# An RWKV-7 block with adaptive norm, followed by a second block, on one Trainium2 core: silu(c) and five modulation sums made a stage earlier, and a 16x16 inverse in another form

## The chip, the cores and the metric

The kernel runs on one core of a Trainium2 chip as a single launch. The metric is device time in microseconds (us); the time before is 2746.52 us, the median of three runs (2742.11 to 2747.39). TensorE (PE in the profile, with its weight loads as PEld), VectorE (DVE), ScalarE (ACT) and GpSimd (POOL) compute; SyncE (SP) issues nearly all DMAs. Each engine works off its own list of instructions in the order in which the program was written, and waits where an operand is not there.

## The reference, cut to what matters

One token block of 256 x 2048 in fp32 goes through a conditioned RWKV-7 block with a feed-forward part, and then through a second block (attention, a gated recurrence, an MLP). The change lies wholly within the first half of the first block:

```python
mod = jax.nn.silu(c) @ ada_w + ada_b                       # 2048 x (6 x 2048)
sh_m, sc_m, g_m, sh_f, sc_f, g_f = split(mod + ada_table)  # six vectors of 2048
h = rms(x) * (1 + sc_m) + sh_m
y = rwkv7(h)                                               # r, k, v, w, a, g products, scan, group norm, @ w_o
x = x + g_m * rms(y)
h = rms(x) * (1 + sc_f) + sh_f                             # then the conv feed-forward part, gated by g_f
```

`sh_m` and `sc_m` are needed before anything else. The other four vectors (2048 x 8192 of `ada_w`, 32 MB) are needed only after `y @ w_o`. Here they are called the modulation sums: 128 units, one for each half h of `c` and each block ch of 128 outputs; 96 of them are made before the feed-forward part. In the scan, 256 steps are done in chunks of 16: for each chunk and head a unit lower triangle of 16 x 16 has to be inverted, 64 such triangles for each group of four heads.

## The kernel before, in words

All products are fp32, made from two halves each of weights and of activations (`hi`, `lo`), three matmuls to a product. A weight comes as a `raw` tile of 512 KB by a DMA on SP's queue (`wdma`, L167), ACT casts its high half (`spl`, L183), DVE subtracts to get the low half (`spl`, L184), and PE multiplies. The list of all weight tiles is fixed, and so many of them are loaded ahead as there are `raw` buffers; each load waits for the buffer that an earlier split gives back.

The stages, by the times of the profiled execution:

- **start** (0 to about 165 us, `start`): `x` is loaded (L709), normed and transposed. At the same time 64 tiles of 512 KB of `ada_w` (`ada`, L451) give `sh_m` and `sc_m` in eight groups of eight, by DVE (L471, L474) and PE (L469). Seven `ada` tiles are in flight.
- **mixes** (to about 217 us, `mixes`): the remaining `r` products in two halves of six weights each (L864 to L866), four low-rank hidden vectors (`hidden`, tanh on ACT at L846), and the token-shift mixes for the next products.
- **jit** (217 to about 630 us, `jit`): eight groups g of four heads each. A group makes its k, v, w, a products (L1043 to L1045) slot by slot; at each of 64 slots the function `pump` takes one step of the three streams of earlier work: s0 (decay, keys; ends in L1079 to L1104 and the tiles `LA`, `LB`), s1 (chunk matrices L1141, the inverse L1170 to L1182, its spread over partitions through DRAM images `imgT` and `imgP` into `Tm` and `Pm`, L1214), s2 (the scan chain, and the group norm at L1287 to L1299).
- **wo** (630 to about 830 us): `y @ w_o` in two halves p = 0, 1 of twelve weights, with the last group's streams between.

The modulation sums are a generator, `ada_sums` (L481). It broadcasts a row of `c` over the partitions into `sb` by a DMA on POOL's queue (L497, 512 KB), makes silu(c) by a tanh on ACT (L500) and a multiply on DVE (L501), and then each step makes one sum: DVE multiplies a 512 KB tile `adat` (L492, a DMA on SP) by `sb` and adds up the row (L507). When the unit's half changes, the row and the silu come again. Where the caller calls `next`, there the step stands in all engines' lists, the loads among them. In `mixes` the number of sums is N0 = 0. In `jit` there are N3 = 61, at the slots of the table `SLOT3` (four in group 0, where two go to the row and the silu, seven in group 1, nine in each later group; the second half's row and silu take two slots of the seventh group). One `adat` tile is in flight. In `wo` the other 35 come by `self.pump(1 + p)` for each weight, with five tiles in flight in `scratch` and `ab`.

The inverse (L1172 to L1178) solves the triangle column by column: for t = 1 to 15 DVE multiplies the t x t corner P by column t of G into `tG` (L1176) and adds up along the row into column t (L1178). At t = 4, 7, 9, 11 and 13 it yields to the other streams. L1182 then transposes the result.

The function `wnext` hands out the split weights; `self.deferred` is a list of small pieces of work that the next `flush` in a product loop emits, in order.

Of the kernel before, what the change touches and what calls it, by code (L numbers as in the profile page):

```python
# [97 lines left out]
class Kern:  # L98
# [8 lines left out]
    ASH = [4, 7, 9, 10]  # L107
    N0 = 0
    N3 = 61
    SLOT3 = [[40, 51, 57, 63], [12, 18, 25, 33, 40, 51, 63]] + [[7, 12, 18, 25, 30, 33, 40, 51, 63]] * 6  # L110

# [369 lines left out]
    def ada_sums(self, units, sb, bufs, half=None, lag=0):  # L481

        nc = self.nc
        nb, nxt = len(bufs), 0

        def load(end):
            nonlocal nxt
            while nxt < min(end, len(units)):  # L490
                h, ch = units[nxt]
                nc.sync.dma_start(out=bufs[nxt % nb], in_=self.A["adat"][h, ch])  # L492
                nxt += 1
        load(nb if half is not None else nb - 1)
        for n, (h, ch) in enumerate(units):
            if h != half:
                nc.gpsimd.dma_start(out=sb, in_=self.A["rows"][4, h * 1024:h * 1024 + 1024].partition_broadcast(128))  # L497
                yield
                t = bufs[(n + nb - 1) % nb]
                nc.scalar.activation(out=t, in_=sb, func=AF.Tanh, scale=0.5)  # L500
                nc.vector.scalar_tensor_tensor(out=sb, in0=t, scalar=1.0, in1=sb, op0=ALU.add, op1=ALU.mult)  # L501
                half = h
                load(n + nb)
                yield
            load(n + nb - lag)
            t = bufs[n % nb]
            nc.vector.scalar_tensor_tensor(out=t, in0=t, scalar=0.5, in1=sb, op0=ALU.mult, op1=ALU.mult,  # L507
                                           accum_out=self.asum[:, h, ch:ch + 1])
            if nb == 1 and n + 1 < len(units) and units[n + 1][0] == h:
                load(n + 2)  # L510
            yield
# [138 lines left out]
    def rwkv(self):  # L650
        nc, A, tc = self.nc, self.A, self.tc
        with ExitStack() as top:
            hidp = top.enter_context(tc.tile_pool(name="hid", bufs=1))
            self.hid = hidp.tile([128, 4, 2, S], F32R, name="hid")
            with tc.tile_pool(name="hpool", bufs=1) as hp:
                self.vec0 = hp.tile([128, NVEC - NV1], F32, name="vec0")
# [45 lines left out]
    def start(self):  # L702
# [5 lines left out]
        for tb in range(2):  # L708
            nc.sync.dma_start(out=x0[:, tb, :], in_=A["x"][tb * 128:tb * 128 + 128, :])  # L709
        self.ada_start(range(8), lambda: wk.tile([128, 1024], F32, tag="ada", bufs=7, name="ada")[:], 7)  # L710
        acc = wk.tile([128, 2, 512], F32, name="acc")
# [99 lines left out]
        pp = prep(0)  # L811
        for g in range(1, 8):
            for i, _ in enumerate(ada(g)):
                if g > 1 or i > self.LAG:
                    next(pp, None)
                product()
            if g == 1:
                for _ in pp:
                    pass
            pp = prep(g)  # L820
# [19 lines left out]
    def mixes(self, xr):  # L840
# [3 lines left out]
        def hidden(i, p, func, scale):  # L844
            t = wk.tile([128, S], F32, tag="lt", bufs=2, name="lt")
            nc.scalar.activation(out=t, in_=p, func=AF.Tanh, scale=scale) if func else nc.scalar.copy(out=t, in_=p)  # L846
            if scale == 0.5:
                nc.vector.tensor_scalar(out=t, in0=t, scalar1=0.5, scalar2=0.5, op0=ALU.mult, op1=ALU.add)
            self.hilo(hid[:, i, 0, :], hid[:, i, 1, :], t)
        sums = self.ada_sums(self.aunits[:self.N0], wk.tile([128, 1024], F32, name="sb")[:],  # L850
                             [wk.tile([128, 1024], F32, name=f"ab{i}")[:] for i in range(4)])
        self.aunits = self.aunits[self.N0:]
        next(sums, None)
        for i in range(4):
            self.deferred.append(lambda i=i: hidden(i, self.lb[i // 2][:, i % 2, :], i != 1, 1.0 if i < 2 else 0.5))
        ps = [self.bank(b, (128, S), "r") for b in (7, 0, 1, 2, 3, 4)]
        for half in range(2):
            for n, ft in enumerate(range(10, 16)):
                hi, lo = self.wnext()
                for k in range(8):  # L860
# [8 lines left out]
                    if k == 5 and n:  # L869
                        self.pump()  # L870
                    if k in (1, 4) and n + half:
                        next(sums, None)
# [72 lines left out]
    def jit(self):  # L945
# [12 lines left out]
        n3 = self.N3  # L958
        ab = self.ab = self.sp.tile([128, 2, 1024], F32, name="ab")
        s3 = self.ada_sums(self.aunits[:n3], ab[:, 0, :], [ab[:, 1, :]])  # L960
        self.aunits = self.aunits[n3:]
# [146 lines left out]
    def s1(self, g):  # L1108
# [64 lines left out]
        nc.vector.memset(P[:].rearrange("p a b -> p (a b)")[:, 0:256:17], 1.0)  # L1173
        for t in range(1, 16):
            tv = tmp[:, 0:t * t].rearrange("p (a b) -> p a b", a=t)
            nc.vector.tensor_tensor(out=tv, in0=P[:, 0:t, 0:t], in1=G[:, 0:t, t].unsqueeze(1).broadcast_to([64, t, t]),  # L1176
                                    op=ALU.mult)
            nc.vector.tensor_reduce(out=P[:, 0:t, t], in_=tv, axis=AX.X, op=ALU.add)  # L1178
            if t in (4, 7, 9, 11, 13):
                yield next(at)  # L1180
# [123 lines left out]
    def wo(self):  # L1304
# [9 lines left out]
        ngm = sum(ch < 16 for _, ch in self.aunits)  # L1314
        self.side = [self.ada_sums(self.aunits, self.ab[:, 0, :], v + [self.ab[:, 1, :]], 1, 1)]
        gate = self.ada_gate(0, "b_gm", "t_gm", self.G, self.Af[:], lambda: self.misc((128, 4, 128), "gr"))
# [12 lines left out]
        for p in range(2):  # L1329
# [6 lines left out]
            for kc in range(12):  # L1336
                if p == 0 and kc < 11:
                    split(kc + 1)
                hi, lo = self.wnext()
                self.pump(1 + p)  # L1340
                if p == 1 and kc % 2 and kc < 10:
# [564 lines left out]
```

## Time and profile before

| what | value |
|---|---|
| median of three runs | 2746.52 us |
| profiled execution | 2750.28 us, of which the span from first to last instruction is 2748.2 us |
| PE busy | 2607.2 us (95% of the span) |
| DVE, ACT busy | 1771.8 us (64%), 1340.5 us (49%) |
| chain that ended last | PE 84%, ACT 6%, DVE 5%, DMA 3%, issue 2% |
| mean granted TensorE clock | 0.981 of full speed |

A granted clock of 1.00 is TensorE's upper level of 2.4 GHz, 0.5 its lower level of 1.2 GHz; a stretch with 0.54 ran almost wholly at the lower one. The share of the whole span says little about a change that touches the first 830 us only: each stage has its own limit, and the stretch, its waits and its chain have to be read apart. From about 830 us on the program is the same before and after.

### The profile page before, as it was taken

How to read it: one execution, taken by the hardware profiler on the slowest of the kernel's cores; microseconds unless marked ns; L12 is line 12 of the kernel's file. 1: busy time of each engine (PE TensorE's matmuls, PEld its weight loads, DVE VectorE, ACT ScalarE, POOL GpSimd, SP SyncE). 2: the span in 40 equal slices, each digit the busy share in tenths (PEclk: the TensorE clock that was granted, in tenths of full speed). 3: DMA queues.
4: the chain of work that ended last, by engine and by line, in shares of the span. 5: the costliest groups of instructions: out<-in, count | busy, mean ns of one | idle time of the engine just before them, and what ended most of it. 6: DMA issues, size and time to landing. Idle time of an engine off the chain costs nothing.

```text
span 2748.2 us, 47787 instructions
## 1 busy us (share of the span) xinstructions
PE 2607.2 (95%) x19345; PEld 2379.6 (87%) x19345; DVE 1771.8 (64%) x2842; ACT 1340.5 (49%) x2202; POOL 60.0 (2%) x98
## 2 busy tenths in 40 slices
PE   6997899998879999999999899998989999999998
PEld 6997788886659999999888799998789999988886
DVE  6976888887777786666555656665554444455555
ACT  3245565664455444444444555555454444444444
POOL 0000111111000000000000000000000000000000
PEclk9998999999989999999999999999999999999999
DMA  9945555556757785555555544443535555555554
GB/s 337 388 143 173 192 193 186 173 186 206 251 184 265 268 273 174 183 183 184 179 195 193 176 156 138 140 145 118 190 132 184 184 184 182 181 194 194 192 194 159
DMA packets 151084, 532.56 MB, mean 194 GB/s; under 512 B 21328, under 2 KB 21712, under 8 KB 149840
## 3 DMA queue, kind: packets, MB, share of 16 engines
q1 hardware_dynamic: 146640, 515.36, 55.5%
q0 software_dynamic: 3936, 12.06, 1.7%
q8 instruction: 151, 2.47, 0.4%
q10 hardware_dynamic: 288, 2.10, 0.2%
q14 instruction: 69, 0.57, 0.1%
HBM read 523.16 MB, written 6.29 MB: 193 GB/s over the span
## 4 chain that ended last, share of the span: by engine, by line
PE 84%; ACT 6%; DVE 5%; DMA 3%; issue 2%; SPq 0%; DVEq 0%; ACTq 0%; POOLq 0%
PE ta L353 7%; PE ta L354 7%; PE ta L352 7%; PE f L274 6%; PE f L276 6%; PE f L275 6%; PE u L274 4%; PE u L275 4%; PE u L276 4%; PE m L1043 3%; PE m L1044 3%; PE m L1045 3%; PE r L776 2%; DVE spl L184 1%; PE mi L1141 1%
## 5 line engine op out<-in xcount | busy, mean ns | idle before, releaser
L184 DVE TENSOR_TENSOR spl<-raw,spl 128x1024 fp32r<-128x1024 f32 x748 | 913.2, 1222 | 776.7 <-ACT spl L183 773.7
L183 ACT CAST spl<-raw 128x1024 fp32r<-128x1024 f32 x748 | 781.3, 1045 | 860.8 <-PE ta L354 307.4
L274 PE MATMUL f<-yhl,spl 128*128 128x256 f32 x1376 | 390.1, 284 | 0.0
L275 PE MATMUL f<-yhl,spl 128*128 128x256 f32 x1376 | 389.7, 283 | 0.0
L276 PE MATMUL f<-yhl,spl 128*128 128x256 f32 x1376 | 389.7, 283 | 0.0
L352 PE MATMUL ta<-spl,shl 128*128 128x512 f32 x832 | 324.8, 390 | 3.4 <-ACT shl L287 3.4
L353 PE MATMUL ta<-spl,shl 128*128 128x512 f32 x832 | 324.6, 390 | 1.5 <-DVE spl L184 1.5
L354 PE MATMUL ta<-spl,shl 128*128 128x512 f32 x832 | 324.4, 390 | 0.0
L274 PE MATMUL u<-hl,spl 128*128 128x256 f32 x1024 | 290.1, 283 | 0.0
L275 PE MATMUL u<-hl,spl 128*128 128x256 f32 x1024 | 290.0, 283 | 0.0
L276 PE MATMUL u<-hl,spl 128*128 128x256 f32 x1024 | 290.0, 283 | 0.0
L275 PEld LDWEIGHTS f<-yhl,spl 128*128 128x128 f32 x1376 | 264.3, 192 | 0.0
L274 PEld LDWEIGHTS f<-yhl,spl 128*128 128x128 f32 x1376 | 264.3, 192 | 0.0
L276 PEld LDWEIGHTS f<-yhl,spl 128*128 128x128 f32 x1376 | 264.3, 192 | 0.0
L1043 PE MATMUL m<-hl,spl 128*128 128x256 f32 x672 | 200.3, 298 | 0.0
L275 PEld LDWEIGHTS u<-hl,spl 128*128 128x128 f32 x1024 | 196.7, 192 | 0.0
L276 PEld LDWEIGHTS u<-hl,spl 128*128 128x128 f32 x1024 | 196.7, 192 | 0.0
L274 PEld LDWEIGHTS u<-hl,spl 128*128 128x128 f32 x1024 | 196.7, 192 | 0.0
L1044 PE MATMUL m<-hl,spl 128*128 128x256 f32 x672 | 190.5, 283 | 0.0
L1045 PE MATMUL m<-hl,spl 128*128 128x256 f32 x672 | 190.5, 283 | 0.0
L352 PEld LDWEIGHTS ta<-spl,shl 128*128 128x128 f32 x832 | 156.6, 188 | 36.5 <-ACT shl L287 3.8
L353 PEld LDWEIGHTS ta<-spl,shl 128*128 128x128 f32 x832 | 156.6, 188 | 34.6 <-DVE spl L184 2.1
(424 smaller groups left out, 4799.3 us busy)
## 6 DMA issues: line engine op xcount, KB each, us to landing
raw<-in_ffn_in SPq DMA_DIRECT2D x172, 512.0 KB, 4.7
raw<-in_w_up SPq DMA_DIRECT2D x128, 512.0 KB, 3.8
raw<-in_w_down SPq DMA_DIRECT2D x128, 512.0 KB, 4.4
raw<-in_ffn_out SPq DMA_DIRECT2D x86, 512.0 KB, 3.8
raw<-in_w_in SPq DMA_DIRECT2D x84, 512.0 KB, 3.7
raw<-in_w_rkv SPq DMA_DIRECT2D x76, 512.0 KB, 4.4
ab<-in_adat SPq DMA_DIRECT2D x68, 512.0 KB, 3.5
ada<-in_ada SPq DMA_DIRECT2D x64, 512.0 KB, 6.6
```

What stands on the lines that cost most here:

```text
L183: self.nc.scalar.copy(out=hi[:, :n], in_=t[:, :n])
L184: self.nc.vector.tensor_tensor(out=lo[:, :n], in0=t[:, :n], in1=hi[:, :n].bitcast(F32), op=ALU.subtract)
L274: nc.tensor.matmul(out, lhsT=hi[:, w], rhs=xhl[:, 0, kc, :], start=(kc == 0), stop=False)
L275: nc.tensor.matmul(out, lhsT=hi[:, w], rhs=xhl[:, 1, kc, :], start=False, stop=False)
L276: nc.tensor.matmul(out, lhsT=lo[:, w], rhs=xhl[:, 0, kc, :], start=False, stop=(kc == KD - 1))
L352: nc.tensor.matmul(o, lhsT=shl[0][:, t0], rhs=hi[:, w], start=first, stop=False)
L353: nc.tensor.matmul(o, lhsT=shl[0][:, t0], rhs=lo[:, w], start=False, stop=False)
L354: nc.tensor.matmul(o, lhsT=shl[1][:, t0], rhs=hi[:, w], start=False, stop=last)
L776: nc.tensor.matmul(out, lhsT=wd[:, w], rhs=xt[:, g % 2, max(0, min(3, ft - 9)), kc % 2, :], start=False, stop=e)
L1043: nc.tensor.matmul(out, lhsT=hi[:, w], rhs=xhl[:, 0, kc, :], start=(kc == 0), stop=False)
L1044: nc.tensor.matmul(out, lhsT=hi[:, w], rhs=xhl[:, 1, kc, :], start=False, stop=False)
L1045: nc.tensor.matmul(out, lhsT=lo[:, w], rhs=xhl[:, 0, kc, :], start=False, stop=(kc == KD - 1))
```

## The change

Seven edits. `sb` becomes a tile of its own that lives through the whole RWKV part, and its row for the first half of `c` is written in `start`, in the code of the sixth modulation group. The silu of this half is put behind the four hidden vectors in `mixes`, and five sums stand in the first half of its weight loop (N0 = 5), with three tiles for `adat`. `ada_sums` yields right after its first loads when it is handed a finished silu; its callers take that first step at once. Group 0 of `jit` has two slots for sums instead of four, and no silu; since 61 units still follow, the change of halves comes earlier, and the second silu falls on the last slot of the sixth group. In `wo` 30 sums are left, and the second half's steps go 1, 2, 1, 2. `start` has six `ada` tiles instead of seven. The inverse gives the same result in another order: the first row is copied from G, and as soon as column t is finished its part is added to all later columns, n x m elements with n = t + 1 and m = 15 - t.

```diff
-    N0 = 0
+    N0 = 5
     N3 = 61
-    SLOT3 = [[40, 51, 57, 63], [12, 18, 25, 33, 40, 51, 63]] + [[7, 12, 18, 25, 30, 33, 40, 51, 63]] * 6
+    SLOT3 = [[46, 62], [12, 18, 25, 33, 40, 51, 63]] + [[7, 12, 18, 25, 30, 33, 40, 51, 63]] * 6
...
         load(nb if half is not None else nb - 1)
+        if half is not None:
+            yield
         for n, (h, ch) in enumerate(units):
...
             self.hid = hidp.tile([128, 4, 2, S], F32R, name="hid")
+            self.sb = hidp.tile([128, 1024], F32, name="sb")
...
-        self.ada_start(range(8), lambda: wk.tile([128, 1024], F32, tag="ada", bufs=7, name="ada")[:], 7)
+        self.ada_start(range(8), lambda: wk.tile([128, 1024], F32, tag="ada", bufs=6, name="ada")[:], 6)
...
         for g in range(1, 8):
+            if g == 5:
+                nc.gpsimd.dma_start(out=self.sb[:], in_=A["rows"][4, 0:1024].partition_broadcast(128))
...
-        sums = self.ada_sums(self.aunits[:self.N0], wk.tile([128, 1024], F32, name="sb")[:],
-                             [wk.tile([128, 1024], F32, name=f"ab{i}")[:] for i in range(4)])
+        sums = self.ada_sums(self.aunits[:self.N0], self.sb[:],
+                             [wk.tile([128, 1024], F32, name=f"ab{i}")[:] for i in range(3)], 0)
...
+        def silu():
+            t = wk.tile([128, 1024], F32, name="st")
+            nc.scalar.activation(out=t[:], in_=self.sb[:], func=AF.Tanh, scale=0.5)
+            nc.vector.scalar_tensor_tensor(out=self.sb[:], in0=t[:], scalar=1.0, in1=self.sb[:], op0=ALU.add,
+                                           op1=ALU.mult)
+        self.deferred.append(silu)
...
-                    if k in (1, 4) and n + half:
+                    if k == 5 and n:
                         next(sums, None)
...
-        ab = self.ab = self.sp.tile([128, 2, 1024], F32, name="ab")
-        s3 = self.ada_sums(self.aunits[:n3], ab[:, 0, :], [ab[:, 1, :]])
+        ab = self.ab = self.sp.tile([128, 1024], F32, name="ab")
+        s3 = self.ada_sums(self.aunits[:n3], self.sb[:], [ab[:]], 0)
+        next(s3)
...
-        for t in range(1, 16):
-            tv = tmp[:, 0:t * t].rearrange("p (a b) -> p a b", a=t)
-            nc.vector.tensor_tensor(out=tv, in0=P[:, 0:t, 0:t], in1=G[:, 0:t, t].unsqueeze(1).broadcast_to([64, t, t]),
-                                    op=ALU.mult)
-            nc.vector.tensor_reduce(out=P[:, 0:t, t], in_=tv, axis=AX.X, op=ALU.add)
-            if t in (4, 7, 9, 11, 13):
+        nc.vector.tensor_copy(out=P[:, 0, 1:16], in_=G[:, 0, 1:16])
+        for t in range(1, 15):
+
+            n, m = t + 1, 15 - t
+            if m > 1:
+                tv = tmp[:, 0:n * m].rearrange("p (a b) -> p a b", a=n)
+                nc.vector.tensor_tensor(out=tv, in0=P[:, 0:n, t:t + 1].broadcast_to([64, n, m]),
+                                        in1=G[:, t, n:16].unsqueeze(1).broadcast_to([64, n, m]), op=ALU.mult)
+                nc.vector.tensor_tensor(out=P[:, 0:n, n:16], in0=tv, in1=P[:, 0:n, n:16], op=ALU.add)
+            else:
+                nc.vector.scalar_tensor_tensor(out=P[:, 0:n, 15], in0=P[:, 0:n, t], scalar=G[:, t, 15:16],
+                                               in1=P[:, 0:n, 15], op0=ALU.mult, op1=ALU.add)
+            if t in (3, 5, 7, 9, 12):
                 yield next(at)
...
-        self.side = [self.ada_sums(self.aunits, self.ab[:, 0, :], v + [self.ab[:, 1, :]], 1, 1)]
+        self.side = [self.ada_sums(self.aunits, self.sb[:], v + [self.ab[:]], 1, 1)]
+        next(self.side[0])
...
-                self.pump(1 + p)
+                self.pump(1 + kc % 2 * p)
```

The instructions themselves move as follows; the line numbers of the changed kernel are some 2 to 20 higher.

VectorE in group 0 before, from the keys of stream s0 to the first chunk matrices' operand `LA`:

```order
L1090 SCALAR_TENSOR_TENSOR kb<-kb,k 128x8x64
L501 SCALAR_TENSOR_TENSOR ab<-ab 128x1024
L1093 TENSOR_TENSOR kkr<-C,kkr 128x512
L1094 SCALAR_TENSOR_TENSOR kb<-za,kkr 128x8x64
L1099 SCALAR_TENSOR_TENSOR C<-r,vec,kb 128x256 x2
L1104 TENSOR_TENSOR kb<-kb,zw 128x1024
L184 TENSOR_TENSOR spl_2139<-raw_2057,spl_2138 128x1024
L507 SCALAR_TENSOR_TENSOR ab,asum<-ab 128x1024 x2
L184 TENSOR_TENSOR spl_2176<-raw_2088,spl_2175 128x1024
L1118 TENSOR_TENSOR LA<-r,Ep 128x8x64
L1119 SCALAR_TENSOR_TENSOR LA<-kkr,Ep 128x8x64
```

The same place on VectorE in the changed kernel:

```order
L509 SCALAR_TENSOR_TENSOR ab,asum<-ab,sb 128x1024
L184 TENSOR_TENSOR spl_2106<-raw_2032,spl_2105 128x1024
L1093 TENSOR_SCALAR C<-mi_2112 128x512
L1100 TENSOR_SCALAR kb<-za,half 128x4x64 x2
L1103 SCALAR_TENSOR_TENSOR kb<-kb,k 128x8x64
L1106 TENSOR_TENSOR kkr<-C,kkr 128x512
L1107 SCALAR_TENSOR_TENSOR kb<-za,kkr 128x8x64
L1112 SCALAR_TENSOR_TENSOR C<-r,vec,kb 128x256 x2
L1117 TENSOR_TENSOR kb<-kb,zw 128x1024
L184 TENSOR_TENSOR spl_2151<-raw_2071,spl_2150 128x1024
L509 SCALAR_TENSOR_TENSOR ab,asum<-ab,sb 128x1024
L184 TENSOR_TENSOR spl_2186<-raw_2103,spl_2185 128x1024
```

The silu (L501) and one of the two sums ahead of `LA` are gone; the other of the two new sums stands a split earlier, and the two `LA` rows follow the last row shown.

ScalarE where the sixth group ends and the seventh begins, before (`VA`, `VB`: chunk values; `v`: the group's values; `LB`: the copied half of `LA`):

```order
L1206 COPY VB<-mi_5286 64x4x64
L981 COPY v<-pv_5029 128x512
L183 CAST spl_5314<-raw_5174 128x1024
L1121 COPY LB<-LA 64x1024
L1123 COPY ecl<-Ep 128x8
```

and in the changed kernel:

```order
L1226 COPY VB<-mi_5284 64x4x64
L502 ACT_TABLE_LOAD
L502 ACTIVATE ab<-sb 128x1024
L994 COPY v<-pv_5028 128x512
L183 CAST spl_5313<-raw_5173 128x1024
```

A table load and the tanh of the second half's silu now stand ahead of the copy of `v` and of the cast. On VectorE the silu's multiply stands at the same place, where a sum was:

```order
L1117 TENSOR_TENSOR kb<-kb,zw 128x1024
L184 TENSOR_TENSOR spl_5244<-raw_5111,spl_5243 128x1024
L503 SCALAR_TENSOR_TENSOR sb<-ab,sb 128x1024
L1314 TENSOR_TENSOR r<-r,Y 128x512
L1317 SCALAR_TENSOR_TENSOR r<-r,vec,bv 128x256
L1319 SCALAR_TENSOR_TENSOR r<-r,vec,zg 128x256
L1317 SCALAR_TENSOR_TENSOR r<-r,vec,bv 128x256
L1319 SCALAR_TENSOR_TENSOR r<-r,vec,zg 128x256
L184 TENSOR_TENSOR spl_5314<-raw_5173,spl_5313 128x1024
```

The five rows of the group norm, a split and the two `LA` rows come behind it.

SyncE's loads where `wo` begins, before (`scratch<-in_rows`: the row of the norm's gain, 1 MB):

```order
L542 DMA scratch<-in_rows 128x2048
L167 DMA raw_6668<-in_w_o 128x1024
L167 DMA raw_6670<-in_w_o 128x1024
L167 DMA raw_6699<-in_w_o 128x1024
L492 DMA scratch<-in_adat 128x1024 x4
L492 DMA ab<-in_adat 128x1024
```

and in the changed kernel:

```order
L544 DMA scratch<-in_rows 128x2048
L492 DMA scratch<-in_adat 128x1024 x4
L492 DMA ab<-in_adat 128x1024
L167 DMA raw_6669<-in_w_o 128x1024
L167 DMA raw_6671<-in_w_o 128x1024
L167 DMA raw_6700<-in_w_o 128x1024
```

Five loads for the sums have moved ahead of three weights. On POOL the row of `c` for the first half, before the first DMA after `start`, is now the first DMA of the program; it waits for nothing. The second half's row stands between the stores of the sixth group's images (`imgT`, `imgP`) and the loads of its `Tm`. On PE the order is the same in both.

## Rows read from the trace of the kernel before

**Rows 1.** Windows: busy us of each engine (instructions), clock, DMA share, GB/s.
```profile
241.00:258.00 17.00, 8.51 (x30) 6.77 (x31) 11.34 (x17) 3.07 (x5) 0.00 (x0) 0.51 0.49 171
305.00:630.00 325.00, 313.40 (x3403) 266.08 (x3402) 282.72 (x548) 201.09 (x406) 42.93 (x67) 0.99 0.56 187
548.20:551.60 3.40, 3.36 (x16) 3.37 (x17) 1.87 (x4) 1.85 (x5) 0.00 (x0) 0.54 0.76 266
647.10:657.40 10.30, 9.00 (x80) 7.51 (x81) 8.41 (x13) 3.27 (x7) 0.00 (x0) 0.51 0.36 103
```

**Rows 2.** Chain of waits, 0 to 20 us: start us, us, what.
```profile
2.13 6.39 DMA x<-in_x
```

**Rows 3.** DMA view, 60 to 120 us.
```profile
DMA packets 6371, 22.32 MB, mean 372 GB/s; under 512 B 704, under 2 KB 704, under 8 KB 6364
```

**Rows 4.** Tile `ada`, 0 to 170 us: count, ns min/median/max, first and last start.
```profile
L451 SPq DMA_DIRECT2D ada<-in_ada x64: 327/328/1147, 3.1 to 130.8; - x64
...
DMA to landing us min/median/max: 3.2/6.6/12.7
```

**Rows 5.** PE's waits, 165 to 211 us: us in total, times, longest.
```profile
PE r L864 <- ACT spl L183: 1.9, 1, 1.9
```

**Rows 6.** VectorE's timeline in mixes: start, us, instruction [idle before <-releaser].
```profile
184.09 1.23 DVE L184 TENSOR_TENSOR spl<-raw,spl 128x1024 fp32r<-128x1024 f32 x1 [3.18 <-ACT spl L183]
```

**Rows 7.** Chain of waits, 215 to 305 us.
```profile
236.88 1.28 ACT L500
238.18 1.06 ACT ab L500
239.26 1.23 DVE ab L501
...
245.01 1.15 DVE ab L507 x2
246.18 3.23 DMA ab<-in_adat
```

**Rows 8.** VectorE by form, 270 to 288 us: busy us, mean ns of one.
```profile
L1176 DVE TENSOR_TENSOR tG<-PG,G 64x225 f32<-64x225 f32 x1 | 0.5, 548 | 0.0
...
L1176 DVE TENSOR_TENSOR tG<-PG,G 64x64 f32<-64x64 f32 x1 | 0.3, 258 | 0.0
```

**Rows 9.** PE's waits, 211 to 305 us.
```profile
PE mi L1214 <- DMA Tm<-imgT: 3.5, 2, 2.3
```

**Rows 10.** Chain of waits, 515 to 524.5 us.
```profile
518.80 0.59 ACT v L981
```

**Rows 11.** VectorE's timeline, 515 to 526 us.
```profile
517.29 0.69 DVE L1294 TENSOR_TENSOR r<-r,Y 128x512 f32<-128x512 f32 x1 [0.43 <-ACT Y L299]
...
520.37 1.23 DVE L184 TENSOR_TENSOR spl<-raw,spl 128x1024 fp32r<-128x1024 f32 x1 [0.43 <-ACT spl L183]
```

**Rows 12.** PE's timeline: three groups' L1079, and L1141 after the sixth group.
```profile
451.15 0.70 PE L1079 MATMUL mi<-C,cst 128*128 128x512 f32 x1
...
506.39 0.70 PE L1079 MATMUL mi<-C,cst 128*128 128x512 f32 x1
...
522.94 1.13 PE L1141 MATMUL mi<-LA,kb 64*128 64x128 f32 x8 [0.45 <-DVE LA L1119]
...
564.39 0.70 PE L1079 MATMUL mi<-C,cst 128*128 128x512 f32 x1
```

**Rows 13.** Chain of waits, 626 to 660 us.
```profile
637.33 6.43 DMA scratch<-in_adat
...
647.82 0.96 ACT spl L183
...
651.83 3.68 PE mi L1214 x64
```

**Rows 14.** VectorE's waits, 625 to 780 us.
```profile
DVE scratch L507 <- DMA scratch<-in_adat: 12.5, 5, 6.9
```

**Rows 15.** PE's waits, 625 to 780 us.
```profile
PE ch L1253 <- DVE Pm L1234: 3.4, 1, 3.4
```

## The prediction, made before the result was known

> **What bounds the kernel now.** I read the windows first, stage by stage, because 95% busy over the whole span hides where PE stands still. In groups 1 to 7 of jit PE works 313.40 of 325 us at a clock of 0.99 [rows 1]: work taken from VectorE or ScalarE there buys nothing unless PE waits for it. The change can only pay or cost where PE does wait, so I then listed PE's waits by stretch and read the chain of waits through each long one. There are five such places below 830 us: the program's start [rows 2], the turn to the second `r` loop in mixes [rows 5], group 0 [rows 7, 9], the second silu [rows 12], and wo [rows 13 to 15]. After a long gap PE also runs for a while at the lower clock: 17 us at 0.51 in group 0, 3.4 us at 0.54 after the second silu, 10.3 us at 0.51 where wo begins [rows 1]. Such a stretch costs about half of its busy time: 4.2, 1.5 and 4.4 us. After 830 us nothing differs.
>
> All sums below are against the profiled execution (2750.28 us, span 2748.2, so 2.1 us lie around it); the median of the runs is 2746.52, 0.14% less, and I carry the difference over to it unchanged.
>
> **1. The row of silu's input at the start: +1.0.** The row's DMA waits for nothing on POOL, so its 512 KB travel with `x`, on whose landing the first work hangs: 6.39 us for the first megabyte [rows 2]. At 372 GB/s [rows 3] 512 KB take 1.4 us. If the queue has room while `x` starts, it costs 0. I take 1.0, nearer to the full price, as everything in the stage hangs behind `x`. That the row is gone from 218 us helps nothing on its own; there the first sum's tile takes its place.
>
> **2. Six tiles instead of seven: 0.** 57 tiles follow the first seven between 3 and 130.8 us, one per 2.24 us [rows 4]; six in flight leave 13.4 us from a tile's issue to its reuse. Landing takes 6.6 us in the median, 12.7 at worst [rows 4]. The worst is in the first rush, where fewer loads in the queue also land sooner. The price if this cover goes is the third rival.
>
> **3. Mixes: +1.2 (0 to +3).** The tanh (1.06) and the multiply (1.23), priced by the old silu [rows 7], stand behind the hidden vectors and ahead of the next split, exactly where PE already waits 1.9 us for a cast [rows 5]. ScalarE pays first, and VectorE's multiply overlaps the next cast, so the delay is the larger of the two, 1.2, not their sum. Below, 0 if something else is later; above, +3 if the longer gap lengthens the lower clock behind it by a stretch like the short one [rows 1]. The table is the one just used by the hidden vectors, so no load. The five sums fall into VectorE's idle time: a split is 1.23 with 3.18 idle before it [rows 6], and a sum takes 1.15 [rows 7]. If that cover were gone, each would cost 1.15.
>
> **4. Group 0: -10.0 (-5 to -14).** The chain runs from the decay's last activation to `LA`, which L1141 on PE reads. Removed from it [rows 7]: table load, tanh and multiply, 236.88 to 240.49 = 3.6; one of two sums, 1.15; the load of the next `adat` tile, 3.23, since with both sums' tiles fetched far earlier nothing is left to land there. That is 8.0. Against it, the first `adat` tile now stands ahead of a weight, worth up to 1.4 at [rows 3]'s rate, partly repaid by the row that no longer travels there: +0.5. PE's gap ahead of L1141 was what kept the clock low for 17 us; of the 4.2 us lost there I count 1.5, the rest lay inside the waits. The new inverse is shorter by 1.5 us (next item), and PE waits 3.5 us for `Tm` behind it [rows 9]: -1.0 of that. Low end: only the load and the sum count (-4.4) and little else; high end: whole clock loss and whole `Tm` wait.
>
> The table load moves to the next group's tanh, where every later group has one already and PE does not wait.
>
> **5. The inverse elsewhere: 0.** Old: 30 small operations; a 64x64 multiply is 0.258, 64x225 0.548, so 1.8 ns per element of a row [rows 8]. New: a copy, 26 operations of 28 to 64 elements and a last one of 15. The fixed part of an operation is 0.258 - 64 x 0.0018 = 0.14. The multiplies fall from 1240 elements to 650: 1.8 ns on 590 is 1.1, and two operations less are 0.3. The reductions give way to additions in place over the same 650; such an addition is not in the trace, and at half the multiply's slope per element more or less than a reduction it moves the sum by 0.6 either way: -0.8 to -2.0. I take -1.5. From group 2 on PE is the bound [rows 1] and this is worth nothing.
> The Trainium skill (VectorE: DVE Perf Modes, Walkthrough: the 8-slice pipeline in each mode) has fp32 tensor_tensor at one element per cycle of 0.96 GHz, 1.04 ns; the row's 1.8 ns does not agree, probably by the pattern of its operands, which I cannot tell. By the skill's rate the new inverse would be an estimated 1 us shorter still and the total 1 us lower.
>
> **6. The second silu at the end of the sixth group: +3.5 (+1.5 to +6.5).** Before, it cost one group 58.00 us from L1079 to L1079 instead of 55.24 [rows 12]: 2.8, which now goes. Its new place is ahead of the copy of `v` at 518.80 [rows 10]. Load 1.28 and tanh 1.06 from there end at 521.2, the multiply at 522.4. The group norm behind it on VectorE, which began at 517.29, therefore starts 5.1 later; its five operations take until 520.0 before [rows 11], now until 525.1; the split at 520.37 starts at 525.1, and so `LA` comes 4.7 later. PE waited 0.45 there already [rows 12], and its list holds nothing else to do: a gap of 5.1. Behind it I count 3.4 us of lower clock, 1.5 [rows 1]. 4.7 + 1.5 - 2.8 = +3.5. Low: part is caught up before the chain products; high: a stretch as at 647 [rows 1], 4.4. The adat load that now waits for the multiply, and the loads of `Tm` behind the row on POOL, come later by 1 to 4 us, but inside the same gap.
> On tables the row shows the tanh 0.02 us after a load of 1.28 [rows 7]. The Trainium skill (ScalarE: Activation LUTs, What ACT_TABLE_LOAD costs) adds a drain of 1.38 us to each switch; the trace does not show it. With it the term would be +4.9 and the total 1.4 higher.
>
> **7. Where wo begins: -3.0 (-6 to 0).** VectorE's first sum waits 6.9 us for its tile [rows 14], issued at 637.33 behind three weights and landed at 643.76 [rows 13], and everything for `LA` queues behind that sum. Now the five tiles go ahead of the three weights. That alone is 3 x 1.4 = 4.2 us [rows 3], the first tile at 639.5; and the issue no longer waits until the third weight has a buffer, so it is rather 2 us less, 637.5 (an estimate). But the first of the weights lands behind the other four tiles, 5 x 1.4 = 7.0 later: 644.5, where before it had long been there. From its cast to PE's L1214 lie 4.0 us (647.82 to 651.83 [rows 13]), so L1214 starts at about 648.5: 3.3 earlier, not 6.9. The stall moves to the weight. I take 3.0. Low: the clock's 4.4 [rows 1] partly comes back too. High: the first tile lands at 640 or later, and the weight with it.
>
> **8. The rest of wo: -4.0 (-8 to 0).** Five sums less here: 5 x 1.15 of VectorE, and 5 x 1.4 = 7.0 us of DMA; the sums' waits besides the first are 12.5 - 6.9 = 5.6 [rows 14], and the longest wait of PE, 3.4 [rows 15], hangs on VectorE behind them. I count it and half a microsecond at the end.
>
> Sum: 1.0 + 0 + 1.2 - 10.0 + 0 + 3.5 - 3.0 - 4.0 = -11.3: 2739.0 profiled, 2735 for the median. Its own range, by errors of the terms that are independent: 2728 to 2742.
>
> **Rivals.**
> A, *the new gap costs far more*: lower clock after the sixth group lasts as in group 0, 17 us and 8 us lost [rows 1] instead of 1.5. For it: the gap, 5.1, is as long as the longest there. Against: there several gaps followed each other. Total -5: 2742.
> B, *the weights take the place of the sums' tiles*: in group 0 and in wo the loads for the sums go ahead of weights; if those are as tight as it seems, items 7 and 8 give 0 and item 4 loses 1.4: -3: 2743.5. For it: item 7's working; against: VectorE waited 12.5 us for sums' tiles [rows 14], which only then counts for nothing.
> C, *slower: six tiles are too few at the start*. One mechanism: a tile that takes longer than 13.4 us from issue to reuse holds up the next; each microsecond above costs 64/6 = 10.7. At 15.0 us it is +17: 2752. It outweighs the gains from 14.5 us. For it: landing can take 12.7 [rows 4]; against: the median of 6.6 leaves 6.8 for use.
> D, *more comes back*: the clock's loss in group 0 and in wo goes whole, 4.2 + 4.4 less the 1.5 counted: 2728 or below.
>
> **How the numbers follow.** Forecast 0.55, A 0.17, B 0.14, C 0.08, D 0.06. A measurement of this kernel tells differences above about 0.2%, 5.5 us: faster means below 2741.0, slower above 2752.0. Faster: nearly all of the forecast (0.53), D, and somewhat under half of A and B (0.14): 0.73. Slower: C at its price and a little of A and B together: 0.07. Same: 0.20. The range 2722 to 2747 leaves out C and the far ends.
>
> **What would show it.** `LA` in group 0 done about 8 us earlier and hardly any time below full clock between 241 and 258 us of before (4); PE waiting some 5 us at L1141 after the sixth group, and a normal seventh group of 55.2 (6); the first sum in wo no longer waiting, but a gap of 3 to 4 us ahead of the first L1214 (7); one load of `ada` at most that VectorE or PE waits for (2). I am wrong if the start stage grows by over 2 us, if the gap in (6) vanishes, or if the first gap in wo stays as it is.

## The result, and the profile after

The changed kernel takes 2732.64 us (median of five runs, 2730.64 to 2738.36) against 2746.52 (2742.11 to 2747.81). The ratio is 0.9941, 95% interval 0.9927 to 0.9956: faster by 16 us, between 12 and 20; the two medians by themselves are 13.9 us apart. The span of the profiled execution fell from 2748.2 to 2728.9.

PE runs the same instructions in the same order in all kernels here, so one instruction, by its number, can be looked up in two traces, and the difference of its two start times is how far the program is ahead (minus) or behind (plus) there. This table has that shift in us (median over the PE instructions within 3 us of the time named, which is a time of before), and the ends of a stage subtracted give what the stage gained or lost. One execution of each kernel stands behind it.

How far executions of the same instructions differ can be read from two runs further down: the one that changes only the loads of wo is off by -1.5 us in mixes, +3.2 in group 0 and -1.4 from 540 to 575, where its program is still that of before; the one that changes only the start by -0.6 in group 0 and -1.7 at wo's beginning. The last 1900 us, the same in all kernels, lie between -3.4 and +1.6. So a stage's figure is good to 2 or 3 us. Group 0 as in the changed kernel is in six runs, and gains between 6.8 and 8.6 in them.

| us of before | 160 | 210 | 305 | 500 | 540 | 575 | 628 | 660 | 760 | 830 | 2740 |
|---|---|---|---|---|---|---|---|---|---|---|---|
| changed kernel, shift | +0.3 | +1.4 | -6.2 | -6.4 | +1.3 | -2.3 | -2.3 | -8.3 | -16.7 | -18.5 | -19.3 |

Stage by stage against the forecast (from the shifts before rounding):

| stage | forecast | measured |
|---|---|---|
| start | +1.0 | +0.3 |
| mixes | +1.2 | +1.0 |
| group 0 (210 to 305) | -10.0 | -7.5 |
| silu at the end of the sixth group, and the old one gone (500 to 575) | +3.5 | +7.6 - 3.5 = +4.1 |
| wo's beginning (628 to 660) | -3.0 | -6.0 |
| rest of wo (660 to 830) | -4.0 | -10.2 |

The windows that answer to [rows 1] (columns as there):

```profile
241.00:258.00 17.00, 15.21 (x78) 12.87 (x79) 13.40 (x20) 4.20 (x8) 1.18 (x2) 0.70 0.42 147
305.00:630.00 325.00, 310.21 (x3343) 263.05 (x3342) 266.49 (x531) 201.80 (x408) 42.48 (x67) 0.98 0.56 185
521.00:528.00 7.00, 6.93 (x77) 6.39 (x78) 5.42 (x9) 2.50 (x4) 0.00 (x0) 0.50 0.43 152
632.00:640.00 8.00, 7.76 (x23) 5.04 (x23) 5.95 (x10) 2.93 (x6) 0.00 (x0) 0.79 1.02 381
640.00:660.00 20.00, 18.40 (x199) 14.23 (x198) 15.27 (x25) 6.47 (x11) 1.39 (x2) 1.00 0.59 202
700.00:760.00 60.00, 58.73 (x514) 43.87 (x513) 43.97 (x68) 27.37 (x51) 0.00 (x0) 1.00 0.72 247
```

In group 0 PE is busy 15.2 of the 17 us in which it had been busy 8.5, partly still at the lower clock. Where wo begins, the lower clock is gone from 640 to 660 us, but a shorter stretch has come ahead of it: 0.79 from 632 to 640, and 0.50 from 634 to 637. The kernel before had 1.00 there. A new stretch of 7 us at 0.50, the lower level of 1.2 GHz, stands at 521 to 528.

The chain through group 0, which answers to [rows 7] (start, us, what):

```profile
239.56 0.80 DVE C L1112 x2
...
241.52 1.23 DVE spl L184
...
246.36 2.00 PE mi L1154 x8
```

From the decay's activations (236.7 to 238.1) on, no table, no tanh, no sum and no load stand on it any more; PE's first product with `LA` (L1154, the old L1141) starts at 246.3 where it started at 253.1. What PE waits for from 211 to 300 us:

```profile
PE mi L1092 <- ACT C L1089: 5.5, 2, 3.0
PE mi L1234 <- DMA Tm<-imgT: 4.0, 1, 4.0
PE pk L1058 <- DVE spl L184: 3.2, 1, 3.2
PE pv L1058 <- DVE spl L184: 1.7, 1, 1.7
```

The wait for `Tm`, 3.5 before [rows 9], has become 4.0, although the program is 7 us ahead and the inverse is shorter.

The end of the sixth group, answering to [rows 10 to 12] (timeline of the changed kernel: start, us, engine, what; in brackets the idle time before it and what ended it). ScalarE first:

```profile
512.42 1.28 ACT L502 ACT_TABLE_LOAD   x1
513.71 1.06 ACT L502 ACTIVATE ab<-sb 128x1024 f32<-128x1024 f32 x1
514.79 0.58 ACT L994 COPY v<-pv 128x512 f32<-128x512 f32 x1
```

The load of the table and the tanh stand right behind each other, and the copy of PE's result `pv` into `v` follows. VectorE beside them:

```profile
514.80 1.22 DVE L503 SCALAR_TENSOR_TENSOR sb<-ab,sb 128x1024 f32<-128x1024 f32 x1 [6.56 <-ACT ab L502]
515.94 0.68 DVE L1314 TENSOR_TENSOR r<-r,Y 128x512 f32<-128x512 f32 x1
...
518.50 1.22 DVE L184 TENSOR_TENSOR spl<-raw,spl 128x1024 fp32r<-128x1024 f32 x1
```

The multiply by the tanh's result stands ahead of the group norm's and the split's operations. PE in the same stretch:

```profile
500.01 1.13 PE L1092 MATMUL mi<-C,cst 128*128 128x512 f32 x2
...
521.07 1.61 PE L1154 MATMUL mi<-LA,kb 64*128 64x128 f32 x6 [4.94 <-DVE LA L1132]
...
562.14 1.13 PE L1092 MATMUL mi<-C,cst 128*128 128x512 f32 x2
```

VectorE stands idle for 6.56 us until the tanh is done, and five operations of the group norm, a split and `LA` follow. PE's wait of 0.45 us there is now 4.94, and the group takes 62.1 us from L1092 to L1092, where the one before it takes 55.2.

The chain of waits where wo begins, answering to [rows 13]:

```profile
627.73 13.78 DMA raw<-in_w_o
...
641.59 1.05 ACT spl L183
...
645.04 0.61 DVE Y L1245
...
645.69 2.29 PE mi L1234 x64
```

A weight, its cast, VectorE's `Y`, which stands behind the weight's split in VectorE's list, and PE's chunk product with `Y` follow one another. In the kernel before, the longest of PE's waits from 625 to 780 us hung on VectorE behind the first sum:

```profile
PE mi L1141 <- DVE bv L1129: 4.2, 1, 4.2
```

It is gone. PE's waits from 620 to 790 us (total us, count, longest), answering to [rows 15]:

```profile
PE wo L352 <- ACT yhl L287: 3.0, 1, 3.0
PE ch L1280 <- ACT VA L1281: 1.6, 4, 0.4
PE mi L1234 <- DVE Y L1245: 1.6, 1, 1.6
```

VectorE's in the same stretch, answering to [rows 14]:

```profile
DVE scratch L509 <- DMA scratch<-in_adat: 0.9, 2, 0.5
```

The sums' waits for their tiles are down from 12.5 us to 0.9. The chain now runs through a weight that takes 13.8 us to land behind the five tiles; PE waits 1.6 us for what hangs on it. The wait of 3.4 at the chain product after `Pm` [rows 15] is gone too.

### The profile page after: what moved, and what is told of

The parts are those of the page before. It is cut to its first block, busy times and chain, and to the rows that moved or that the text cites. A ratio compares the mean times of both kernels' runs of the same rounds, so it can differ in the third digit from the quotient of the medians.

```text
span 2728.9 us, 47766 instructions
## 1 busy us (share of the span) xinstructions
PE 2602.8 (95%) x19345; PEld 2375.2 (87%) x19345; DVE 1754.7 (64%) x2826; ACT 1341.4 (49%) x2202; POOL 59.5 (2%) x98
## 4 chain that ended last, share of the span: by engine, by line
PE 85%; ACT 6%; DVE 4%; DMA 3%; issue 2%; SPq 0%; POOL 0%; DVEq 0%; ACTq 0%; POOLq 0%
PE ta L353 7%; PE ta L352 7%; PE ta L354 7%; PE f L276 6%; PE f L274 6%; PE f L275 6%; PE u L276 5%; PE u L274 5%; PE u L275 5%; PE m L1056 3%; PE m L1057 3%; PE m L1058 3%; PE mi L1234 1%; PE r L779 1%; PE mi L1154 1%
```

## The experiments

Ratios are to the kernel before. The theories: W, the gain comes from the waits in group 0 and in wo; against it I, the inverse pays in every group.

**The inverse alone.** Edit on the kernel before, cut to its loops (the new inverse whole, and nothing else):

```diff
-        for t in range(1, 16):
...
+        nc.vector.tensor_copy(out=P[:, 0, 1:16], in_=G[:, 0, 1:16])
+        for t in range(1, 15):
...
```

> The kernel before with the new 16x16 inverse and nothing else. Theory W (the gain comes from what stood ahead of PE's products in group 0 and in wo; the inverse is shorter, but PE is the bound or its images come late anyway): VectorE's inverse 1 to 2 us shorter per group, total -1 us, between 0 and -2.5 (ratio 0.9991 to 1.0000). Rival I (the inverse pays in every group, 8 x 1 to 2 us, and is most of the gain): -8 us or more (ratio 0.997 or below).

Measured: 1.0002 (0.9992 to 1.0012). VectorE's groups of the inverse, all eight together, in the kernel before (busy us, mean ns):

```profile
L1176 DVE TENSOR_TENSOR tG<-PG,G 64x1 f32<-64x1 f32 (+14 forms) x120 | 35.4, 295 | 13.7 <-DMA G<-au 10.6
...
L1178 DVE TENSOR_REDUCE PG<-tG 64x1 f32<-64x1 f32 (+14 forms) x120 | 27.9, 232 | 4.3 <-DVE tG L1176 0.3
```

The same groups with the new inverse:

```profile
L1182 DVE TENSOR_TENSOR PG<-tG,PG 64x28 f32<-64x28 f32 (+6 forms) x104 | 21.1, 203 | 3.6
L1180 DVE TENSOR_TENSOR tG<-PG,G 64x28 f32<-64x28 f32 (+6 forms) x104 | 20.9, 201 | 2.8
```

63.3 us became 42.0 and a copy and a last step of 0.17 and 0.24 per group: 2.3 us less per group, and no gain in time that shows. The images show where it went. Median time from issue to landing, in the 15 us around them, in the kernel before (last column, us):

```profile
Tm<-imgT POOLq DMA_DIRECT2D x2, 128.0 KB, 4.1
...
imgT<-tG POOLq DMA_DIRECT2D x1, 64.0 KB, 2.8
```

And with the new inverse alone:

```profile
Tm<-imgT POOLq DMA_DIRECT2D x2, 128.0 KB, 6.2
...
imgT<-tG POOLq DMA_DIRECT2D x1, 64.0 KB, 4.1
```

The store of the image was issued 1.1 us earlier (286.62 for 287.75), closer behind the loads of a sum and a weight (285.4 and 285.8 in both), and took longer; the loads of `Tm` were issued at the same time as before (290.98 for 290.86), now beside the next such pair (290.60 and 291.03) instead of ahead of it (291.74 and 292.17), and landed later. Executions of the old inverse differ too, but less: `Tm` took 5.4 us in the run with only wo's loads changed and 4.0 in the one with six tiles.

**The changed kernel with the old inverse** (the same edit the other way).

> The changed kernel with the inverse of before. Theory W: it keeps nearly the whole gain, -12 to -15 us against before (ratio 0.9945 to 0.9956). Rival I: at least half the gain is lost, -7 us or less (0.9975 or above).

Measured: 0.9952 (0.9940 to 0.9965), 2735.18 us. Nearly the whole gain stays. I is refuted by the pair; two or three microseconds for the inverse within the changed kernel lie inside the intervals.

**Only the loads of wo first.** Edit on the kernel before:

```diff
         load(nb if half is not None else nb - 1)
+        if half is not None:
+            yield
...
         self.side = [self.ada_sums(self.aunits, self.ab[:, 0, :], v + [self.ab[:, 1, :]], 1, 1)]
+        next(self.side[0])
```

> The kernel before, with the five loads for the sums issued ahead of the three weights where wo begins; 35 sums and the old pace of steps stay. Theory W: the first sum no longer waits 6.9 us for its tile, L1141 of the last group comes 4 us earlier and the stretch at the lower clock behind it goes: -6 us, between -4 and -8, all of it between 642 and 660 us of before (ratio 0.9971 to 0.9985). Rival B (the weights take the place of the sums' tiles): the gap moves whole to the weights' casts, 0 to -2 us.

Measured: 0.9984 (0.9974 to 0.9993). The shift goes from +0.6 at 628 us to -5.6 at 660: 6.2 gained at the place named. 1.2 of it are given back by 830 us, where the wait of 3.4 at the chain product [rows 15] is still 2.1:

```profile
PE ch L1255 <- DVE Pm L1236: 2.1, 1, 2.1
```

The whole, 4.4 us by the ratio, is at the low end of W's 4 to 8. Its interval, 1.9 to 7.1, touches the 2 that B allows, the 6.2 at the place named do not: rival B, here and in the prediction, is out.

**The loads of wo last, in the changed kernel.**

```diff
-        next(self.side[0])
...
-                self.pump(1 + kc % 2 * p)
+                self.pump(1 + kc % 2 * p + (p == 0 and kc == 0))
```

> The changed kernel with the five loads of wo behind the three weights again, as before; 30 sums and the new pace stay. Theory W (place of the loads and number of the sums count apart): the first sum waits 6 us and more for its tile again, 6 us come back at wo's beginning, the second half of wo stays as good; +5 to +7 against the changed kernel (ratio to before 0.996 to 0.997). Rival: the two are one effect, and with fewer sums the place does not count: 0 to +2 (0.994 to 0.9955).

Measured: 0.9955 (0.9942 to 0.9969), 2737.42 us, with 0.1 us gained between 628 and 660 instead of 6.0, and 9.7 after it. VectorE's waits in this run, 620 to 790 us:

```profile
DVE scratch L509 <- DMA scratch<-in_adat: 7.3, 1, 7.3
```

PE's waits in the same stretch:

```profile
PE mi L1154 <- DVE bv L1142: 3.0, 1, 3.0
...
PE mi L1234 <- DVE Y L1245: 2.9, 1, 2.9
```

PE's two waits of before (4.2 and 1.3 us) are back, and the later stretch is nearly as good as in the changed kernel (9.7 against 10.2): two separate effects. By time alone this would not be told: +3.8 us by the ratios and +4.8 by the medians fall short of W's +5 to +7, and 0.9955 is the edge of the rival's range. The trace decides against the rival, since the loss stands at wo's beginning alone.

**35 sums in wo, at the old pace.** Edit on the changed kernel:

```diff
-    N3 = 61
+    N3 = 56
...
-                self.pump(1 + kc % 2 * p)
+                self.pump(1 + p)
```

> The changed kernel with N3 = 56 instead of 61 and the old pace of steps in wo, so that wo has 35 sums again, as before, with their loads still ahead of the weights. Theory S (the sums' number and pace in wo cost the second half of wo 9 us, by loads that come too late for VectorE): the 9 us between 660 and 780 us come back, +7 to +10 against the changed kernel (ratio to before 0.9966 to 0.998), with waits of VectorE on tiles of 4 us and more and a PE gap of about 3 us at the chain product after Pm. Rival P (the waits went because wo starts earlier and its streams meet the loads in another phase): 0 to +2 against the changed kernel (0.994 to 0.995).

Measured: 0.9964 (0.9951 to 0.9977), 2739.78 us. Between 660 and 830 us nothing is gained (shift -8.4 to -8.4). VectorE waits 4.9 us for tiles of the sums, its wait from 630 to 800 us:

```profile
DVE scratch L509 <- DMA scratch<-in_adat: 4.9, 3, 2.6
```

PE's waits there, 2.3 us of them at the chain product:

```profile
PE ch L1273 <- DVE Pm L1254: 2.3, 1, 2.3
PE mi L1234 <- DVE Tm L1251: 2.1, 1, 2.1
```

The loss against the changed kernel, 6.3 us by the ratios and 7.1 by the medians, is at the low edge of what S expected, and P's 0 to +2 is out.

**The old pace alone.** Only the second of these two edits; 30 sums.

> The changed kernel with the old pace of steps in wo's second half, two for each weight instead of one and two in turn; 30 sums, which then end six weights earlier. Theory N (the number of the sums counts): at most +2 us against the changed kernel (ratio to before 0.994 to 0.9955). Rival V (the pace counts: two loads and two sums for each weight are more than the queue and VectorE carry there): most of what 35 sums at this pace cost, +5 to +9 (0.996 to 0.9975).

Measured: 0.9960 (0.9947 to 0.9973), 2738.36 us. The stretch 660 to 830 gains 5.1 (-4.9 to -10.0), half of the changed kernel's 10.2, and until 760 us it gains 0.9. VectorE waits 5.7 us for tiles, and the old gap is back:

```profile
PE ch L1273 <- DVE Pm L1254: 3.2, 1, 3.2
```

So the pace is worth about 5 us, 3.2 of them the wait at the chain product, and the five sums less about 5, at the end, where 30 sums are over and 35 are not. The median lost 5.7 us against the changed kernel, 5.2 by the ratios: the low end of what V expected, and more than N's 2.

**The silu elsewhere.** Edit on the changed kernel:

```diff
-    N0 = 5
+    N0 = 7
```

> The changed kernel with seven sums instead of five in mixes (N0 = 7), so that 28 are left in wo and the second half's silu falls two slots of sums earlier, in the midst of the sixth group, where the table of the tanh is loaded already. Theory J (the silu at the end of the sixth group costs a gap of 4 to 5 us at L1141 and a stretch at the lower clock behind it, 6.9 us in all): -5 to -7 us against the changed kernel, so -19 to -21 against before (ratio 0.992 to 0.9935), and the gap at L1141 after the sixth group gone. Rival K (PE is the bound there over the whole group, and the gap is only moved, or two more sums in mixes delay the second loop by as much): 0 to -2 us against the changed kernel (ratio 0.9935 to 0.995).

Measured: 0.9913 (0.9900 to 0.9925), 2723.72 us, 9 us faster than the changed kernel by the medians and 7.7 by the ratios, a little more than J's 5 to 7. The shift stays at -3.9 from 500 to 540 us. PE's timeline at the old gap:

```profile
519.04 1.13 PE L1154 MATMUL mi<-LA,kb 64*128 64x128 f32 x8 [0.45 <-DVE LA L1132]
```

The window behind it (columns as in [rows 1]):

```profile
518.00:526.00 8.00, 7.55 (x105) 6.80 (x105) 7.02 (x12) 2.92 (x6) 0.00 (x0) 1.00 0.38 132
```

The gap of 4.9 us is 0.45 as before, the clock stays up, and the silu costs nothing where it now stands: its tanh runs at 497.4 us without a load, since the decay's tanh has loaded the table at 486.9, and VectorE does the multiply in the place of a sum. J holds, K is refuted. Which counts more, the place or the load that it saves, no run separates. The two further sums in mixes cost nothing that shows (from 160 to 210 us the program falls 1.1 us behind, +2.6 to +3.7, as in the changed kernel, +0.3 to +1.4).

**One further.** `N0 = 8`, which puts the silu right behind the tanh of decay and gate.

> The changed kernel with eight sums in mixes, so that the second half's silu stands at the slot right behind the two tanh of the decay and the key gate in the sixth group, and wo has 27 sums. Theory J (the silu has to stand where its table is loaded and VectorE has slack; sums in mixes are free): like the run with seven, 0.9913, or 1 us better through one sum less in wo (0.990 to 0.992). Rival: eight sums in mixes delay the second loop, or the slot lies on the keys' chain: 2 us and more worse than with seven (0.992 or above).

Measured: 0.9906 (0.9890 to 0.9921), 2724.91 us: the same as with seven, as J said; the sum less in wo shows nothing.

**The first silu alone.** The changed kernel with `N0 = 0`, group 0's sums at slots 57 and 63 as before, and the inverse and wo of before.

> The kernel before with the first half's silu made in mixes (and its row at the program's start, six tiles there), nothing else: no sums in mixes, two sums in group 0 at their old slots, so the second half's silu, the inverse and wo stay as they were. Theory G (in group 0 the silu and the wait for the second sum's tile count apart: 3.6 and 3.2 us): PE's L1141 of the first chunk 3 to 4 us earlier, +2 us at the start and in mixes, in all -1 to -3 us (ratio 0.999 to 0.9996). Rival H (the silu alone is what held group 0; the tile would have been there had the first sum come earlier): -6 us or more (0.998 or below).

Measured: 1.0001 (0.9991 to 1.0012). The chain in group 0:

```profile
243.75 1.15 DVE ab L509 x2
244.92 3.26 DMA ab<-in_adat
...
251.83 2.07 PE mi L1154 x8
```

L1154 comes at 251.8 in place of 253.1, with the program 2.1 us late at 210 us: 3.3 us gained, and the load of 3.26 still there. From 254 to 265 us 2.6 of it go again. That cannot be put down to the silu: the kernels with the inverse alone and with wo's loads alone, which change nothing there, lose 2.4 and 2.7 at the same place, with the clock at 0.91 from 258 to 282 us (0.90 here), where the one execution of the kernel before had 0.99. G was right about the place. The sum, between -2.5 and +3.3 us, is not told apart from G's -1; H is out. What the earlier sum and its landed tile give in group 0 beyond this no run shows by itself; it rests on the chain of waits.

**Six tiles alone.** On the kernel before, `bufs=6` and 6 ahead.

> The kernel before with six tiles in flight in the start stage instead of seven. Theory: nothing, 0 to +1 us (ratio 0.9995 to 1.0005); tiles land before they are needed. Rival C (a tile's turn takes over 13.4 us): each microsecond above costs 10.7, so +5 us or more (1.002 or above).

Measured: 0.9995 (0.9985 to 1.0004). Nothing; rival C is out.

**No sum's load behind the first inverse.** Edit on the run with seven sums:

```diff
-    SLOT3 = [[46, 62], [12, 18, 25, 33, 40, 51, 63]] + ...
+    SLOT3 = [[46, 62], [7, 12, 18, 25, 30, 33, 63]] + ...
```

> The changed kernel with seven sums in mixes, and the seven sums of the second group at slots 7, 12, 18, 25, 30, 33, 63 instead of 12, 18, 25, 33, 40, 51, 63, so that no load for a sum is issued while the first inverse's images are stored and read back. Theory Q (the inverse gains nothing since its images queue behind loads): image to Tm 3 us shorter, PE's wait for Tm in group 0 down from 4 us to 1 to 2, total -2 to -3 us against the run with seven sums (ratio to before 0.990 to 0.9908). Rival: the weights' loads fill the queue all the same, or the earlier sums delay VectorE: 0 to +2 us (0.991 to 0.992).

Measured: 0.9901 (0.9886 to 0.9916), 2722.44 us, the fastest here. PE's wait for `Tm` from 211 to 300 us:

```profile
PE mi L1234 <- DMA Tm<-imgT: 0.4, 1, 0.4
```

The loads of `Tm` (issue to landing, us, last):

```profile
Tm<-imgT POOLq DMA_DIRECT2D x2, 128.0 KB, 3.0
```

3.0 us to landing in place of 6.2, and the wait is gone. No load of 512 KB was issued between 280.0 and 287.6 us, while `Tm`'s loads were issued at 283.7. The interval overlaps that of the run with seven sums, so the gain of 1 to 3 us in total is not told apart by time alone. In the trace group 0 gains 13.0 us instead of 7.5 (the program is 8 us further ahead at 305 us, but 2.3 of these lie in a faster start); 3.2 of them are given back by 308 us, so that about 2 us more than with seven sums are left at 500 us.

**The same with the old inverse.**

> The run with free images, but with the inverse of before. Theory Q (the inverse is on PE's path in group 0 only once nothing else fills the queue behind it): the images are stored 2.3 us later, and PE's wait for Tm grows from 0.4 by 1.5 to 2.5 us; total +2 us (ratio to before 0.9905 to 0.9912). Rival: the wait stays below 1 us, the inverse is off the path there too; 0 (0.990).

Measured: 0.9919 (0.9905 to 0.9933), 2728.38 us. PE's wait for `Tm`:

```profile
PE mi L1227 <- DMA Tm<-imgT: 2.7, 2, 2.3
```

2.3 us more, the time by which the new inverse is shorter: with the sums' loads moved away it is on PE's path, as Q said. By time the two differ by 4.9 us (ratios), more than Q's 2, with intervals that overlap; the wait is the clearer reading.

## Why the prediction was right, step by step

The time fell into the forecast's own range (2728 to 2742 for 2732.6), and the signs of all steps held. The sizes were off in both directions, and the errors cancelled only in part: in the traces the stages add up to -18.5 us at 830 us, not to -11.3, and the profiled execution took 2730.64 us, where 2739.0 was forecast. That the median is nonetheless 2.4 us from the forecast is partly luck: the profiled execution of before (2750.28) was slower than all five timed ones, and that of the changed kernel the fastest of its five. Rival D came true in part, in wo; B and C were refuted by runs, and A's 17 us of lower clock were 7.

- **Start and six tiles (1, 2).** +0.3 instead of +1.0; `x` landed 1.5 us later, but most of it was caught up by 22 us. In the ten kernels here with the row at the start the stage cost between -0.1 and +2.7, about +1 in the middle, so the price was right and this execution a cheap one. Six tiles cost nothing, shown alone; but the first six landed after 9.6 to 12.6 us in that run, the first seven of the kernel before after 9.2 to 12.7: that fewer land sooner did not hold.
- **Mixes (3).** +1.0 against +1.2, at the cast named.
- **Group 0 (4).** `LA` 8 us earlier was right: L1154 moved by 6.8 us, from 1.4 late. Forecast -10.0, measured -7.5. Up to L1154 the step was sound, 8.1 gained for 7.5 forecast; the rest failed: of the 1.5 counted for the clock 0.2 came by 290 us (the clock of the stretch came back only to 0.70), and the wait for `Tm`, which I expected to shrink by 1.0, grew to 4.0 and cost 0.8. How much of the 2.5 is truly missing stays open: the changed group 0 is much alike in six runs, but the old one was 3.2 us slower in the run with only wo's loads changed.
- **Inverse (5).** I had 1.5 us per group and measured 2.3, and priced it at nothing outside group 0, which held. That it would bring 1.0 in group 0 failed: the images stand among loads of 512 KB, and the gain came only with these moved. The Trainium skill (VectorE: DVE Perf Modes, Walkthrough: the 8-slice pipeline in each mode) has 1.04 ns per element for such a multiply. Here 64x28 took 177 ns and 64x64 219, 1.17 ns per element, so for the new form this rate was nearer than the 1.8 ns of the old form's rows.
- **Second silu (6).** A gap of 5.1 was forecast, 4.94 measured, 4.5 more than before for the 4.7 counted. The clock behind it stayed low for 7 us (521 to 528) instead of 3.4; the group lost 6.9 us in all (62.1 less 55.2) where 6.2 were forecast, and so +3.5 became +4.1. The 2.8 us of the old silu were those of one execution: behind its gap of 2.2 us the clock was at 0.54, but 1.00 in three other runs, where it cost 1.4 less. The drain that the Trainium skill (ScalarE: Activation LUTs, What ACT_TABLE_LOAD costs) puts behind a table load is absent again: load at 512.42 for 1.28, tanh at 513.71.
- **wo's beginning (7).** The stall did move to the weight behind the five tiles, and from its cast to L1234 it took 4.1 us, as worked out. Relative to 628 us L1234 came 3.8 us earlier, for 3.3 worked out. PE waited only 1.6 us for it, since it was itself 1.7 us later at that place (shift -2.3 at 632, -0.6 at 640), by the new stretch at 0.50 there. The remaining 2.2 us are the lower clock behind 647 us, which went, and which I had put at nothing in the sum and kept for the low end. In the eight other kernels with these loads first, with the new pace or not, the stage gained between 3.4 and 7.9.
- **Rest of wo (8).** The step that was most mis-sized, -4.0 for -10.2. The sum had counted one wait of PE, 3.4, and half a microsecond for the five sums. The pace, two loads and two sums for each weight against one and two in turn, is worth 5 of the 10 us with 30 sums; I had not priced it as an edit of its own. The five sums are worth the other 5 at the old pace.

What stays open: why stages with the same instructions vary by 1 to 3 us between executions, and why the clock falls behind a gap of 2 to 3 us in one execution and not in another. The -0.8 of the stretch from 830 to 2740 us is within that variation.

## What to carry to other kernels

Price a moved activation by what VectorE and PE have queued behind its result, not by its own length: 2.3 us of table and tanh cost 7.6 us at a junction, and the tanh alone nothing some twenty slots earlier, where the table was loaded. A shorter operation gained nothing here while the small DMAs behind it ran among large loads; look at these loads first, then shorten. Where side work is fed into a product loop, its pace is a price of its own: here one and two steps in turn against two for each weight were worth 5 us of 170.

## What the runs showed of the hardware that was not expected

The store of a 64 KB image and its reading back as 128 KB took 2.8 and 4.1 us (before), 4.1 and 6.2 (the inverse alone), or 4.6 and 3.0 (the sums' loads moved away):

```profile
imgT<-tG POOLq DMA_DIRECT2D x1, 64.0 KB, 4.6
```

What differs is which loads of 512 KB were issued beside them. After a gap of 4.94 us PE ran at half its clock for 7 us of continuous work; after one of 1.6 us in wo it stayed at 1.00. In between the same gap went either way: behind 2.96 us ahead of wo's first product the clock was at 0.50 from 634 to 637 us in the changed kernel, and at 1.00 in the kernel before; behind 2.2 us at the old silu it was at 0.54 for 3.4 us in the kernel before, and at 1.00 in the runs with the inverse alone, wo's loads alone and the first silu alone. A price of the lower clock that is read from one trace is the price of that execution.
